# Rope tables of a hybrid transformer layer: their last operations on a scratch unit taken in the ninth pair

## The chip, the cores and the metric

One core of a Trainium2 chip. The metric is device time in microseconds of one execution of the whole layer. Its engines run queues of their own: TensorE (PE, with PEld for its weight loads), VectorE (DVE), ScalarE (ACT), GpSimd (POOL) and SyncE (SP, which issues the loads).

## The reference

One layer on x (1 x 512 tokens x 1024, float32): a half-weighted SwiGLU feed-forward block (width 2816), a mixing stage with two groups of heads, a second half-weighted SwiGLU block, a final RMSNorm. Cut to what matters:

```python
x = x + FFN_RES * swiglu(rms_norm(x, ffn1_norm[l]), ffn1_w_gate[l], ffn1_w_up[l], ffn1_w_down[l])
u = rms_norm(x, mix_norm[l]) @ w_in[l]
c_q, c_kv, k_rope, mq, mk, mv = jnp.split(u, cuts, axis=-1)
a_out = mla_attention(c_q, c_kv, k_rope, positions, ...)      # 8 heads, rotary part of 32
b_out = moba_attention(mq..., mk..., mv..., positions)        # 8 heads, ALiBi
x = x + jnp.concatenate([a_out, b_out], axis=-1) @ w_out[l]
x = x + FFN_RES * swiglu(rms_norm(x, ffn2_norm[l]), ...)
return rms_norm(x, final_norm)

def apply_rope(x, pos):
    inv = jnp.power(ROPE_BASE, -jnp.arange(half) * 2.0 / r)
    ang = pos[:, :, None, None] * inv
    cos, sin = jnp.cos(ang), jnp.sin(ang)
    ...
```

The rope tables are the cosines and sines of position times frequency, for 512 positions and 16 frequencies: 128 partitions of 4 x 16 values. Positions are an input, so the tables are computed on the chip: the angle is reduced to the range from -pi to pi in several pieces, clipped to ±3.1415925, and the sine taken of it (for the sine) and of pi/2 - |angle| (for the cosine).

## The kernel before

Every float32 matrix product is done as three products of a high and a low half: ACT copies a weight chunk of 128 x 1024 into the high half (line 251, in `split`), DVE or POOL subtracts to get the low half (line 252), and PE multiplies (`mm3`, or line 485 in `product`). SP loads the chunks from HBM (line 236).

The up and gate matrices of a feed-forward block are done in `gate_up`: a first piece in `fm_half`, and then ten pairs, each of seven `product`s of 24 matmuls (a scheme with seven products of blocks instead of eight). Before a product, `pump` writes down the splits of the chunks of up to four products ahead; between products `pair` evacuates the banks on ACT (line 495) and DVE (lines 511 to 527), with a Silu on ACT (lines 514, 525). The sums of weight blocks that the scheme wants are DVE's (lines 292 to 300).

Scratch comes from `scr`, nine units of 128 x 512 in one tile. `ualloc` takes the unit at the head of the free list, `ufreeit` puts one back at its tail. Unit 8 is set aside for `blk`, the block of rope tables. Each pair takes three units, called u1, u5 and u2 (with their contents s1, s5 and s2), and gives all three back.

Work that no product needs at once is given as a generator in `aside`; every `product` ends with `tick(2)`, which runs two of its steps. `gate_up` of the first block puts `rope_tables` there when the fourth pair begins (j == 3); ahead of its last part it steps idly until `state["late"]`, which is set from the ninth pair on (j >= 8). It holds one unit for all its 64-column pieces (a, t2, t1, n, p, q, z, y). Nearly all of it is on POOL: the angles (line 794), the reduction in pieces (lines 832 to 849 with the helper lines 787, 788), the clip (line 852). The last part is |a| on DVE (line 857), pi/2 - |a| on POOL (line 859), three Sines on ACT (lines 862, 864, 866), a negation and a memset on POOL (lines 868, 870). The tables are first read in the mix stage, in `c_evac` and `rope_transpose`.

The program so written is not the order of the queues: a planner, when the program is built, orders each engine's instructions by its own estimate of when each can start, keeps what depends on data and on buffers, gives earlier lines of the program precedence, and puts semaphores between engines. On the chip each engine runs its queue in that order.

Of the kernel before, what the change touches and what calls it, by code (L numbers as in the profile page):

```python
# [14 lines left out]
AF = mybir.ActivationFunctionType  # L15
OP = mybir.AluOpType
# [24 lines left out]
def _cut(v):  # L41
    b = np.array([v], np.float32).view(np.uint32) & 0xfffff000
    return float(b.view(np.float32)[0])
# [9 lines left out]
def layer_kernel(ctx, tc, xt, xtok, pos_row, pos_tok, gains, fin, consts, w, wc, out):  # L53
    nc = tc.nc
    V, A, G, T = nc.vector, nc.scalar, nc.gpsimd, nc.tensor
# [90 lines left out]
    def ualloc():  # L146
        u = ufree.popleft()
        return u, scr[:, u * 512:(u + 1) * 512]

    def ufreeit(u):  # L150
        ufree.append(u)
# [627 lines left out]
    blk = scr[:, (NU - 1) * 512:].rearrange("p (t c) -> p t c", t=4)  # L779

    def rope_tables():
        u, sc = ualloc()
        tl = [sc[:, i * 64:i * 64 + 64] for i in range(8)]
        a, t2, t1, n, p, q, z, y = tl

        def STT(o, a_, c, b_, op0, op1):
            G.tensor_scalar(y, a_, c, 1.0, op0=op0, op1=OP.mult)
            G.tensor_tensor(o, y, b_, op=op1)

        pf = sm[:, 68:72]  # L790
        V.tensor_copy(pf, pi)
        yield 1
        v3 = a.rearrange("p (t f) -> p t f", t=4)
        G.tensor_tensor(v3, pf[:, :, None].to_broadcast([128, 4, 16]),
                        cst[:, None, CINV - C0:CINV - C0 + 16].to_broadcast([128, 4, 16]), op=OP.mult)
        yield 1

        def reduce(x):
            G.tensor_scalar(n, x, 1.0 / _P, MAGIC, op0=OP.mult, op1=OP.add)
            yield 1  # L800
            G.tensor_scalar(n, n, -MAGIC, 1.0, op0=OP.add, op1=OP.mult)
            yield 1
            for c in (PI_A, PI_B, PI_C):
                STT(x, n, -c, x, op0=OP.mult, op1=OP.add)
                yield 1

        def fold(t, x, step):

            d = math.fmod(step, _P)
            d = d - _P if d > math.pi else d  # L810
            da = _cut(d)
            db = _cut(d - da)
            dc = d - da - db
            G.tensor_scalar(n, t, da / step / _P, MAGIC, op0=OP.mult, op1=OP.add)
            yield 1
            G.tensor_scalar(n, n, -MAGIC, 1.0, op0=OP.add, op1=OP.mult)
            yield 1
            G.tensor_scalar(x, t, da / step, 1.0, op0=OP.mult, op1=OP.mult)
            yield 1
            STT(x, n, -PI_A, x, op0=OP.mult, op1=OP.add)  # L820
            yield 1
            STT(x, t, db / step, x, op0=OP.mult, op1=OP.add)
            yield 1
            STT(x, n, -PI_B, x, op0=OP.mult, op1=OP.add)
            yield 1
            STT(x, t, dc / step, x, op0=OP.mult, op1=OP.add)
            yield 1
            STT(x, n, -PI_C, x, op0=OP.mult, op1=OP.add)
            yield 1

        m2, m1 = MAGIC * 2.0 ** 21, MAGIC * 2.0 ** 12
        G.tensor_scalar(t2, a, m2, 1.0, op0=OP.add, op1=OP.mult)
        yield 1
        G.tensor_scalar(t2, t2, -m2, 1.0, op0=OP.add, op1=OP.mult)
        yield 1
        G.tensor_tensor(a, a, t2, op=OP.subtract)
        yield 1
        G.tensor_scalar(t1, a, m1, 1.0, op0=OP.add, op1=OP.mult)
        yield 1
        G.tensor_scalar(t1, t1, -m1, 1.0, op0=OP.add, op1=OP.mult)  # L840
        yield 1
        G.tensor_tensor(a, a, t1, op=OP.subtract)
        yield 1
        yield from reduce(a)
        yield from fold(t1, p, 2.0 ** 12)
        yield from fold(t2, q, 2.0 ** 21)
        G.tensor_tensor(p, p, q, op=OP.add)
        yield 1
        G.tensor_tensor(a, a, p, op=OP.add)
        yield 1  # L850
        yield from reduce(a)
        G.tensor_scalar(a, a, 3.1415925, -3.1415925, op0=OP.min, op1=OP.max)
        yield 1

        while not state["late"]:
            yield 1
        V.scalar_tensor_tensor(z, a, -1.0, a, op0=OP.mult, op1=OP.max)
        yield 1
        G.tensor_scalar(z, z, -1.0, math.pi / 2, op0=OP.mult, op1=OP.add)
        yield 1  # L860
        z3 = z.rearrange("p (t f) -> p t f", t=4)
        A.activation(blk[:, :, 64:80], z3, AF.Sin)
        yield 1
        A.activation(blk[:, :, 80:96], z3, AF.Sin)
        yield 1
        A.activation(blk[:, :, 112:128], v3, AF.Sin)
        yield 1
        G.tensor_scalar(blk[:, :, 96:112], blk[:, :, 112:128], -1.0, 1.0, op0=OP.mult, op1=OP.mult)
        yield 1
        G.memset(blk[:, :, 0:64], 1.0)  # L870
        yield 1
        ufreeit(u)
# [8 lines left out]
    def dist_tables():  # L881
# [30 lines left out]
        for i in range(4):  # L912
# [10 lines left out]
            yield 1  # L923

    gate_up(c_f1, c_s1, start_mid0, start_mid1, rope_tables)
    down(c_d1, 8)
    close_part()
# [495 lines left out]
    for t in range(4):  # L1423
        u, xg = ualloc()
        v = v0[:, t:t + 1]
        for n, (a, b) in enumerate(parts[t]):
            for c in last:
# [3 lines left out]
                                   op0=OP.mult, op1=OP.add)  # L1431
# [8 lines left out]
        w1, w2, y, z = tv[:, t:t + 1], tv[:, 4 + t:5 + t], rstd[:, t:t + 1], tt[:, t:t + 1]  # L1440
# [103 lines left out]
```

## Time and profile before

| | |
|---|---|
| median of three runs | 953.11 us (951.67 to 954.19) |
| profiled execution, its own time | 952.19 us |
| span of that execution | 950.4 us |
| mean granted TensorE clock | 0.989 |
| PE busy, share of the span | 920.2 us, 97% |
| DVE busy | 748.6 us, 79% |
| ACT busy | 517.4 us, 54% |
| POOL busy | 116.7 us, 12% |

The span runs from the first to the last instruction; the execution's own time has 1.8 us more around it. Busy times are sums over the whole span; the span is cut into 40 slices of 23.8 us in the page's second part, where a digit is the busy share of a slice in tenths. A wait is named as "engine, line waiting <- engine, line that released it".

### The profile page before, as it was taken

The page shows a single profiled execution, that of the slowest core. Times are in us where ns is not written, and L with a number is a line of the kernel's source. Part 1 is how long each engine was busy: PE and PEld are TensorE (multiplying, and loading weights), DVE is VectorE, ACT ScalarE, POOL GpSimd, SP SyncE. Part 2 cuts the span into 40 slices and gives each one's busy share as a digit, 9 for nine tenths or more (in the row PEclk, how much of TensorE's full clock was granted, in tenths as well). Part 3 has the DMA queues.
Part 4 walks back from the last instruction along what each step waited for, and adds up shares of the span by engine and source line. Part 5 has one row for each costly group of instructions (what it writes and reads, how often), then busy time and mean ns, then how long its engine had stood idle before and what let it go on. Part 6 is the DMA issues. An engine that isn't in the chain of part 4 may idle for free.

```text
span 950.4 us, 15102 instructions
## 1 busy us (share of the span) xinstructions
PE 920.2 (97%) x5901; PEld 838.1 (88%) x5901; DVE 748.6 (79%) x1090; ACT 517.4 (54%) x832; POOL 116.7 (12%) x173
## 2 busy tenths in 40 slices
PE   8993999999999999999999999999999999999997
PEld 6993999999988888998787888899999999988886
DVE  6984989879988956445688887689798879988845
ACT  7643544545636525455787865655455544735524
POOL 2053000000000000011756730000000000000001
PEclk9997999999999999999999999999999999999999
DMA  9420433224603424132434362123233323610302
GB/s 329 174 89 24 133 112 112 90 91 152 220 5 100 118 89 138 62 126 72 152 121 152 125 195 98 45 69 109 90 93 127 114 89 112 221 67 26 109 0 89
DMA packets 38088, 105.41 MB, mean 111 GB/s; under 512 B 4480, under 2 KB 11264, under 8 KB 38016
## 3 DMA queue, kind: packets, MB, share of 16 engines
q1 hardware_dynamic: 37008, 102.61, 33.2%
q10 hardware_dynamic: 1008, 1.84, 0.5%
q8 instruction: 46, 0.75, 0.3%
q14 instruction: 26, 0.21, 0.1%
HBM read 90.40 MB, written 2.10 MB: 97 GB/s over the span
## 4 chain that ended last, share of the span: by engine, by line
PE 46%; ACT 2%; DVE 1%; POOL 1%; DMA 1%; issue 0%; ACTq 0%; SPq 0%; DVEq 0%; POOLq 0%
PE bank L485 21%; PE bank L326 7%; PE bank L328 7%; PE bank L327 7%; PE bank L1190 2%; PE bank L1172 1%; POOL scr L1143 1%; ACT scr L1135 1%; DMA ext<-scr 0%; PE bank L402 0%; ACT ar L251 0%; DMA ar<-scr 0%; DVE ext L1176 0%; ACT ar L1175 0%; POOL ext L1259 0%
## 5 line engine op out<-in xcount | busy, mean ns | idle before, releaser
L485 PE MATMUL bank<-ar 128*128 128x256 f32 x3360 | 406.6, 284 | 16.6 <-DVE scr L516 16.0
L485 PEld LDWEIGHTS bank<-ar 128*128 128x128 f32 x3360 | 405.2, 193 | 17.7 <-DVE scr L516 16.4
L251 ACT ACTIVATE ar<-raw 128x1024 fp32r<-128x1024 f32 (+3 forms) x182 | 177.0, 982 | 155.3 <-issue 45.5
L326 PE MATMUL bank<-ar 128*128 128x512 f32 (+4 forms) x664 | 255.3, 385 | 2.6 <-ACT ar L251 2.2
L328 PE MATMUL bank<-ar 128*128 128x512 f32 (+4 forms) x664 | 253.7, 382 | 0.0
L327 PE MATMUL bank<-ar 128*128 128x512 f32 (+4 forms) x664 | 253.6, 382 | 0.0
L252 DVE TENSOR_TENSOR ar<-raw,ar 128x1024 fp32r<-128x1024 f32 (+2 forms) x164 | 192.0, 1181 | 53.9 <-ACT ar L251 35.8
L326 PEld LDWEIGHTS bank<-ar 128*128 128x128 f32 x664 | 124.8, 188 | 25.9 <-ACT ar L251 2.6
L328 PEld LDWEIGHTS bank<-ar 128*128 128x128 f32 x664 | 125.1, 188 | 23.3
L327 PEld LDWEIGHTS bank<-ar 128*128 128x128 f32 x664 | 125.2, 188 | 22.4 <-DVE ar L390 0.2
L251 ACT ACTIVATE ar<-sq 128x1024 fp32r<-128x1024 f32 x62 | 65.6, 1058 | 77.4 <-DVE sq L295 27.1
L252 DVE TENSOR_TENSOR ar<-sq,ar 128x1024 fp32r<-128x1024 f32 x62 | 75.6, 1220 | 26.8 <-ACT ar L251 26.8
L1409 POOL TENSOR_TENSOR x<-x,tabs 128x512 f32<-128x512 f32 x4 | 5.2, 1288 | 353.6 <-ACT scr L354 353.6
L1143 POOL TENSOR_SCALAR scr<-scr,sm 128x128 f32<-128x128 f32 (+1 forms) x64 | 41.1, 662 | 41.4 <-DVE sm L1140 40.5
L617 DVE SCALAR_TENSOR_TENSOR x<-bank,sm,x 128x512 f32<-128x512 f32 x37 | 27.0, 747 | 23.8 <-PE bank L328 23.8
L1135 ACT ACTIVATE scr<-scr,sm 128x256 f32<-128x256 f32 (+1 forms) x64 | 35.3, 553 | 16.9 <-DVE sm L1127 16.8
L495 ACT ACTIVATE scr<-bank 128x512 f32<-128x512 f32 x60 | 34.9, 581 | 6.7 <-PE bank L485 6.7
L354 ACT ACTIVATE scr<-x 128x512 f32<-128x512 f32 x28 | 17.5, 631 | 29.2 <-DVE x L617 27.0
L948 POOL MEMSET ext<- 64x512 f32 x6 | 3.3, 547 | 215.0 <-DVE ar L252 214.5
L575 ACT ACTIVATE ar<-h 128x512 fp32r<-128x512 f32 x28 | 17.3, 630 | 17.1 <-PE bank L327 8.8
L252 POOL TENSOR_TENSOR ar<-raw,ar 128x512 fp32r<-128x512 f32 x18 | 24.1, 1351 | 9.2 <-ACT ar L251 8.3
L295 DVE TENSOR_TENSOR sq<-sq,raw 128x1024 f32<-128x1024 f32 x20 | 24.5, 1223 | 0.5
(239 smaller groups left out, 926.8 us busy)
## 6 DMA issues: line engine op xcount, KB each, us to landing
raw<-in_w_dram SPq DMA_DIRECT2D x144, 512.0 KB, 3.5
h<-in_w_dram SPq DMA_DIRECT2D x8, 512.0 KB, 3.5
ext<-scr SPq DMA_DIRECT2D x13, 256.0 KB, 2.4
raw<-in_wc_dram SPq DMA_DIRECT2D x8, 336.0 KB, 3.3
ext<-scr SPq DMA_DIRECT2D x13, 192.0 KB, 2.3
x<-in_xtok_dram SPq DMA_DIRECT2D x4, 512.0 KB, 8.2
ext<-scr SPq DMA_DIRECT2D x16, 128.0 KB, 2.1
xs<-in_xt_dram SPq DMA_DIRECT2D x5, 256.0 KB, 5.0
```

The lines of the kernel that those rows point to most:

```text
L251: A.activation(sl(h)[:, a:b], src[:, a:b], AF.Copy)
L252: (e or V).tensor_tensor(sl(l)[:, a:b], src[:, a:b], slf(h)[:, a:b], op=OP.subtract)
L295: V.tensor_tensor(sq, sq, r(q11), op=OP.subtract)
L326: T.matmul(ps, lhsT=ah, rhs=bh, start=start, stop=False, **kw)
L327: T.matmul(ps, lhsT=ah, rhs=bl, start=False, stop=False, **kw)
L328: T.matmul(ps, lhsT=al, rhs=bh, start=False, stop=stop, **kw)
L485: T.matmul(o, lhsT=a_[:, ws], rhs=b_[:, xs_], start=first and e == 0 and k == 0 and n == 0, stop=k == 3 and n == 2, skip_group_check=True)
L495: A.activation(t, banks[b], AF.Copy)
L617: V.scalar_tensor_tensor(xs, banks[b], r, xs, op0=OP.mult, op1=OP.add)
L1135: A.activation(p, p, AF.Exp, scale=-1.0, bias=mn[z][:, i:i + 1], accum_out=rs[z][:, i:i + 1])
L1143: G.tensor_scalar(p, p, ri[z][:, i:i + 1], 1.0, op0=OP.mult, op1=OP.mult)
L1190: T.matmul(banks[b][:, 128 * j:512], lhsT=vw, rhs=pr[:, o:o + n], start=(j == 0 and e == 0), stop=(j == 3 and e == 1))
```

## The change

The name z for the seventh piece of the old unit goes. The clip, which wrote a in place and stood ahead of the loop that waits for the ninth pair, moves behind that loop, and writes to a piece e of a unit that is taken there (u2 in the generator, not the u2 of a pair). |e| and pi/2 - |e| are made in a second piece of that unit, and the second of the two operations goes from POOL to DVE. The third Sine reads e instead of a. The new unit is given back behind the third Sine, the old one at the end as before.

```diff
-        a, t2, t1, n, p, q, z, y = tl
+        a, t2, t1, n, p, q, _, y = tl
...
         yield from reduce(a)
-        G.tensor_scalar(a, a, 3.1415925, -3.1415925, op0=OP.min, op1=OP.max)
-        yield 1
 
         while not state["late"]:
             yield 1
-        V.scalar_tensor_tensor(z, a, -1.0, a, op0=OP.mult, op1=OP.max)
-        yield 1
-        G.tensor_scalar(z, z, -1.0, math.pi / 2, op0=OP.mult, op1=OP.add)
-        yield 1
-        z3 = z.rearrange("p (t f) -> p t f", t=4)
+        u2, sc = ualloc()
+        e, z = sc[:, 0:64], sc[:, 64:128]
+        e3, z3 = (x.rearrange("p (t f) -> p t f", t=4) for x in (e, z))
+        G.tensor_scalar(e, a, 3.1415925, -3.1415925, op0=OP.min, op1=OP.max)
+        yield 1
+        V.scalar_tensor_tensor(z, e, -1.0, e, op0=OP.mult, op1=OP.max)
+        yield 1
+        V.tensor_scalar(z, z, -1.0, math.pi / 2, op0=OP.mult, op1=OP.add)
+        yield 1
         A.activation(blk[:, :, 64:80], z3, AF.Sin)
         yield 1
         A.activation(blk[:, :, 80:96], z3, AF.Sin)
         yield 1
-        A.activation(blk[:, :, 112:128], v3, AF.Sin)
-        yield 1
+        A.activation(blk[:, :, 112:128], e3, AF.Sin)
+        yield 1
+        ufreeit(u2)
         G.tensor_scalar(blk[:, :, 96:112], blk[:, :, 112:128], -1.0, 1.0, op0=OP.mult, op1=OP.mult)
```

## The prediction

> **What bounds the kernel now.** The page first: its head, busy times and slices.
>
> ```profile
> span 950.4 us, 15102 instructions
> ...
> PE 920.2 (97%) x5901; PEld 838.1 (88%) x5901; DVE 748.6 (79%) x1090; ACT 517.4 (54%) x832; POOL 116.7 (12%) x173
> ...
> PE   8993999999999999999999999999999999999997
> ...
> PEclk9997999999999999999999999999999999999999
> ```
>
> TensorE is busy for 97% of the span, so time can come only from the 30 us in which it is not. One slice stands out, the fourth (71 to 95 us): PE busy 3 tenths, granted clock 7 tenths. The waits of PE say how much of the 30 us is one wait, the first row here:
>
> ```profile
> PE bank L485 <- DVE scr L516: 16.0, 2, 15.1
> PE bank L326 <- ACT ar L251: 2.2, 1, 2.2
> ```
>
> Half of PE's idle time is a single wait of 15.1 us in the first feed-forward block. The timeline of all engines there tells its cause; the number in brackets is the idle time ahead of a row and what ended it:
>
> ```profile
> 54.79 0.68 DVE L517 TENSOR_TENSOR h<-scr 128x512 f32<-128x512 f32 x1
> ...
> 55.56 1.20 POOL L794 TENSOR_TENSOR scr<-sm,cst 128x64 f32<-128x64 f32 x1 [41.69 <-DVE h L517]
> ...
> 61.95 1.40 POOL L842 TENSOR_TENSOR scr<-scr 128x64 f32<-128x64 f32 x1
> ...
> 62.26 0.60 ACT L495 ACTIVATE scr<-bank 128x512 f32<-128x512 f32 x1 [0.70 <-PE bank L485]
> ...
> 67.90 1.34 DVE L297 TENSOR_TENSOR raw<-raw,raw 128x1024 f32<-128x1024 f32 x1
> 68.25 1.10 POOL L787 TENSOR_SCALAR scr<-scr 128x64 f32<-128x64 f32 x1
> 69.43 0.32 POOL L788 TENSOR_TENSOR scr<-scr 128x64 f32<-128x64 f32 x1
> ...
> 82.71 0.24 POOL L852 TENSOR_SCALAR scr<-scr 128x64 f32<-128x64 f32 x1
> 82.98 0.26 ACT L866 ACTIVATE scr<-scr 128x64 f32<-128x64 f32 x1 [20.13 <-POOL scr L852]
> 83.15 1.04 ACT L251 ACTIVATE ar<-sq 128x1024 fp32r<-128x1024 f32 x1
> ...
> 84.22 1.23 DVE L252 TENSOR_TENSOR ar<-sq,ar 128x1024 fp32r<-128x1024 f32 x1 [14.97 <-ACT ar L251]
> ...
> 85.36 0.69 DVE L516 TENSOR_TENSOR scr<-bank,scr 128x512 f32<-128x512 f32 x1
> ...
> 86.10 26.13 PE L485 MATMUL bank<-ar 128*128 128x256 f32 x204 [15.12 <-DVE scr L516]
> ...
> 99.60 0.22 DVE L857 SCALAR_TENSOR_TENSOR scr<-scr 128x64 f32<-128x64 f32 x1
> ...
> 99.91 1.15 POOL L859 TENSOR_SCALAR scr<-scr 128x64 f32<-128x64 f32 x1 [16.34 <-DVE scr L857]
> 101.09 0.26 ACT L862 ACTIVATE scr<-scr 128x64 f32<-128x64 f32 x1 [1.31 <-POOL scr L859]
> ```
>
> Three things are to be read here. First, the engines' queues are not in program order: the rope generator starts in the fourth pair of the code and its Sin L866 is written in the ninth, yet POOL starts the tables at 55.56, as soon as DVE L517 of the first pair has let go of the scratch unit, and ACT holds L866 already in the second pair. The planner pulls an operation forward as far as its data and its buffer allow. Second, each queue runs in its order: ACT has nothing to show from 62.86 (62.26 + 0.60) to 82.98, because L866 stands at its head and waits for the clip L852 at the end of POOL's chain. Third, the chain of the stall: clip, Sin, ACT's weight copy L251, DVE's subtraction L252, DVE's bank evacuation L516, and the seventh product of the second pair, which adds to that bank. DVE idles 14.97 us and PE 15.12 us, for one operation of 0.26 us that nobody needs before the mix stage.
>
> **The change, part by part.** *The clip and the third Sin.* Before, the clip wrote its own unit, so only the POOL chain held it. Now it writes a unit taken when the ninth pair's first product has been written down. Followed through the code, the free list (nine units, one set aside for the table block, one held by the rope scratch, three taken and given back by each pair) then has at its head number 7, last used as s1 of the sixth pair, whose last reader is L527 of that pair. L527 writes to the h tiles in the first six pairs only, so the last of these is the one:
>
> ```profile
> L527 DVE TENSOR_TENSOR h<-bank,scr x6: 677/686/692, 61.4 to 173.5; 128x512 f32<-128x512 f32 x6
> ```
>
> As L794 waited for L517, the clip must now wait for this L527, at 173.5 in the old time, some 158 in the new. No Sin can be pulled ahead of the clip, since all three read what it writes. The stall at 71 us therefore loses its cause.
>
> *What of the 15.12 us comes back.* What is late next is DVE itself, which was busy up to 69.24 (67.90 + 1.34). Without the Sin, L251's input from DVE is there and L252 follows at 69.24 where it stood at 84.22: everything behind it moves by 14.97 us or so, L516 ends at 71.1 and PE, done at 70.98 (86.10 - 15.12), waits 0.14 us instead. Gain: 14.98 us.
>
> *The clock after the gap.* The windows (length, then busy time of PE, PEld, DVE, ACT, POOL, then granted clock, DMA share, GB/s):
>
> ```profile
> 55.00:71.00 16.00, 15.98 (x134) 15.77 (x132) 14.24 (x15) 5.51 (x7) 14.01 (x19) 1.00 0.40 132
> 71.00:86.00 15.00, 0.00 (x0) 0.00 (x0) 1.78 (x3) 2.67 (x4) 9.42 (x35) 0.65 0.00 1
> 86.00:90.00 4.00, 3.90 (x21) 3.90 (x22) 4.00 (x6) 1.06 (x1) 0.00 (x0) 0.59 0.36 113
> 90.00:94.00 4.00, 4.00 (x36) 4.00 (x35) 3.17 (x5) 3.10 (x5) 0.00 (x0) 1.00 0.06 23
> ...
> 152.00:252.00 100.00, 100.00 (x834) 99.96 (x833) 89.59 (x101) 55.36 (x71) 0.00 (x0) 1.00 0.43 137
> ...
> 86.10:251.62 165.52, 165.52 (x1367) 165.52 (x1368) 147.97 (x163) 88.42 (x110) 1.15 (x1) 0.99 0.39 124
> ```
>
> and, from the chain that ended last, the second block, which runs the same ten pairs with no rope tables beside them:
>
> ```profile
> 638.25 192.95 PE bank L485 x1608
> ```
>
> The clock falls to 0.59 and is back at 1.00 from 90 us on. The second block needs 192.95/1608 = 0.1200 us a matmul; the 1368 after the gap (1680 in ten pairs of seven products of 24, less the thirteen products up to the gap) should take 164.16 us and took 165.52. So 1.36 us more go with the gap. TensorE: Matmul & The Clock Gate (Part 1: The HAM clock gate) of the Trainium skill says that an idle window of about 3.4 us drops the clock to half, and about as long a busy one restores it; an estimate by that figure is half of 3.4, 1.7 us, which would put the result 0.34 us lower. The second block's row also shows no stall in the same code with nothing of the tables in the queues.
>
> *POOL's chain beside a busy DVE.* From 69.24 to 84.22 DVE stood idle, and POOL's operations took 0.24 to 0.32 us; beside DVE they had taken up to 1.40 (L842). After the change DVE does not stop. Of the chain, 14 operations lay before 69.35 (to the end of L787 at 68.25) and 37 before the clip come after: 5 up to 71 us (19 - 14), and 32 of the second window's 35, less one on the border, L868 and the clip. At the early pace, (69.35 - 55.56)/14 = 0.985 us, they end at 106 us; at 1.40 us each plus 0.1 between them, at 125. Both are well ahead of 158. What they cost DVE, by its groups in 55 to 69 us (with POOL) and in 102 to 250 us (without):
>
> ```profile
> L252 DVE TENSOR_TENSOR ar<-raw,ar 128x1024 fp32r<-128x1024 f32 x4 | 5.0, 1286 | 0.0
> L297 DVE TENSOR_TENSOR raw<-raw,raw 128x1024 f32<-128x1024 f32 x2 | 2.6, 1280 | 0.0
> ...
> L252 DVE TENSOR_TENSOR ar<-raw,ar 128x1024 fp32r<-128x1024 f32 x32 | 38.8, 1220 | 4.3 <-ACT ar L251 4.3
> ...
> L297 DVE TENSOR_TENSOR raw<-raw,raw 128x1024 f32<-128x1024 f32 x6 | 7.3, 1221 | 0.1
> ```
>
> 4 x 0.066 + 2 x 0.059 = 0.38 us for 14 POOL operations, 0.027 each: 1.0 us for 37. From above, L297 at 67.90 took 1.34, 0.12 longer: 4.4 us for 37. DVE idles 10.4 us of 100 with the pairs at full speed (152 to 252), 3.8 us in the chain's 36, so PE loses between 0 and 0.6 us. I take 0.4, nearer the upper end because DVE enters this stretch with no lead (busy without a break up to 69.24).
>
> *The last operations at their new place.* The clip moves behind L527; SP's queue is not passed, no DMA moves. POOL has nothing else in its queue till the mix stage. ACT's Sins may wait for the clip, or for DVE's second step, as L862 did at 101.09: 1.31 us, PE at work throughout. Behind a waiting Sin are ACT's copies, then DVE's subtractions, then products several steps on. Bounds 0 and 1.31 us; I take 0, because that row cost PE nothing. The z step goes from POOL (1.15) to DVE, where its neighbour L857 took 0.22: it fits in DVE's 10.4 us. The three Sins, the memset and the negation stay as many.
>
> *The free list.* One more unit is out for part of a pair that needs three of seven. The order differs through the down projection and is the same four units (7, 6, 8, 5) where attention starts. Cost 0.
>
> Sum on the profiled execution: 952.19 - 14.98 - 1.36 + 0.4 = 936.25 us. The median shown, 953.11, is 0.92 above that execution; so 937.2 us.
>
> **The rivals.** *VectorE becomes the bound while the chain runs.* For it, PE's other wait on L516, at the end of the first pair, where DVE had no slack either:
>
> ```profile
> 53.80 17.18 PE L485 MATMUL bank<-ar 128*128 128x256 f32 x141 [0.85 <-DVE scr L516]
> ```
>
> Against: 0.027 us an operation. If DVE stood still for every POOL operation at its undisturbed 0.32 us, 37 cost 11.8, less 3.8 of slack: 8.0 us instead of 0.4, 944.8. It decides from 0.1 us an operation up. SBUF — State Buffer (SBUF: two separate sides) of the Trainium skill speaks for this: the port pair of the two engines is locked for a whole instruction and the loser blocks fully. By that the trace agrees for POOL (0.24 against 1.40) and shows little of it for DVE.
>
> *The wait moves instead of going.* ACT's order is fixed by a planner that thought the chain finished soon after 62.86 and was 20 us off. If a Sin stands in the sixth or seventh pair ahead of what releases it, ACT stops again; with one operation left on POOL, not 52, the error is 1.15 us and a hand-over, 1.31 us as at L862, on ACT and once more for DVE's steps: 2.6 us, 939.8; a gap over that would need an order that I cannot see, up to 950.
>
> *The change does not do it:* if the unit were free at 82 us already, clip and Sin would stay put: 953.1. It would take a unit last used in the second pair; the list gives the sixth.
>
> *Slower.* If POOL's chain still ran when L527 of the sixth pair is through, Sin L866's successor would hold ACT as before, and longer: to lose 3 us against now, the stall must pass 18 us, the chain end after 175 us, and its 37 operations take (175 - 69.4)/37 = 2.9 us each, twice the longest row. Time then 956 or more.
>
> **How the numbers follow.** Forecast 0.74 (934 to 939.5). VectorE bound 0.09 (939.5 to 945). The wait moved 0.09 (939.5 to 950). No effect 0.04. Slower 0.04. A run of this kernel is told from no change beyond about 0.3%, 2.9 us: faster 0.91, same 0.05, slower 0.04. Range 934 to 943: it leaves out the upper parts of the two partial rivals and the last two cases, some 0.17.
>
> **What would show it.** PE's waits should have no entry above 2.5 us; the fourth slice should read 9 for PE and clock; L252 should run at about 69 us without idle time before it; POOL's chain should last till 95 to 125 us with operations of about 1 us; POOL's clip should be released by DVE L527 near 158 us, the Sins after it. The prediction is wrong if a Sin holds ACT for over 3 us anywhere, if the new PE idle time in the second to fourth pair passes 2 us, or if stages behind the first block, which I take as unmoved, change their length.

## The result, and the profile after

The changed kernel takes 936.03 us (median of four runs, 934.88 to 936.12) against 952.75 of the kernel before (four runs, one more than in the table ahead): a ratio of 0.9822, 95% interval 0.981 to 0.9833. The forecast was 937.2. The profiled execution took 936.12 us, 16.07 less than the one before it; the sum made for that execution was 936.25.

The page of the changed kernel, the lines that answer to those shown of before:

```profile
span 934.3 us, 15098 instructions
...
PE 918.2 (98%) x5901; PEld 835.8 (89%) x5901; DVE 751.7 (80%) x1091; ACT 518.0 (55%) x832; POOL 138.7 (15%) x172
...
PE   8999999999999999999999999999999999999997
...
PEclk9999999999999999999999999999999999999999
```

The hole in the fourth slice is gone from PE's row and from the clock's. POOL is 22 us busier with one instruction less: its operations are the same but for the one that went to DVE, and now they run beside a DVE at work. PE's longest waits in the whole span are these:

```profile
PE bank L326 <- DVE ar L1261: 1.4, 2, 1.0
PE bank L326 <- ACT ar L251: 1.3, 1, 1.3
...
PE bank L485 <- DVE scr L516: 0.8, 1, 0.8
```

The wait of 15.1 us for L516 has left the list; what remains under that name is the first pair's 0.8. The timeline of the changed kernel, from its views by engine, shows the new order (lines behind 852 have moved: the clip is L858, |e| L860, pi/2 - |e| L862, the third Sine L868):

```profile
67.23 1.06 ACT L251 ACTIVATE ar<-sq 128x1024 fp32r<-128x1024 f32 x1 [4.57 <-DVE sq L292]
...
67.70 1.34 DVE L297 TENSOR_TENSOR raw<-raw,raw 128x1024 f32<-128x1024 f32 x1
68.96 1.25 DVE L252 TENSOR_TENSOR ar<-sq,ar 128x1024 fp32r<-128x1024 f32 x1
70.14 0.68 DVE L516 TENSOR_TENSOR scr<-bank,scr 128x512 f32<-128x512 f32 x1
...
53.60 181.58 PE L485 MATMUL bank<-ar 128*128 128x256 f32 x1508 [0.83 <-DVE scr L516]
...
102.70 1.17 POOL L788 TENSOR_TENSOR scr<-scr 128x64 f32<-128x64 f32 x1
157.71 2.21 POOL L858 TENSOR_SCALAR scr<-scr 128x64 f32<-128x64 f32 x1 [53.84 <-DVE h L527]
159.95 0.26 ACT L868 ACTIVATE scr<-scr 128x64 f32<-128x64 f32 x1 [1.03 <-POOL scr L858]
159.95 0.23 DVE L860 SCALAR_TENSOR_TENSOR scr<-scr 128x64 f32<-128x64 f32 x1
160.21 0.20 DVE L862 TENSOR_SCALAR scr<-scr 128x64 f32<-128x64 f32 x1
```

DVE goes from L297 to L252 without a pause where it stood for 14.97 us. PE runs from 53.60 to the end of the block, 1508 matmuls, with no entry in its waits. POOL's chain ends at 103.87. The clip waits 53.84 us on an engine that has nothing else to do, and is let go by DVE L527 of the sixth pair at 157.7. ACT waits 1.03 us for it, and nothing follows from that.

Where the time came from: in the first block from PE's restart in the first pair to the end of the tenth, 181.41 us (53.60 to 235.01) against 197.82 (53.80 to 251.62), 16.41 less. That is the wait of 15.12 and 1.29 more. Ahead of it 0.20 us were gained; the first block's down projection and the mix stage gave 0.51 us back (378.08 us from 235.01 to 613.09, against 377.57); and the second block's pairs and the tail did not change: 321.21 us in both.

### The profile page after: what moved, and what is told of

It reads as the page before. It is cut to its first block, busy times and chain, and to the rows that moved or that the text cites. A ratio compares the mean times of both kernels' runs of the same rounds, so it can differ in the third digit from the quotient of the medians.

```text
span 934.3 us, 15098 instructions
## 1 busy us (share of the span) xinstructions
PE 918.2 (98%) x5901; PEld 835.8 (89%) x5901; DVE 751.7 (80%) x1091; ACT 518.0 (55%) x832; POOL 138.7 (15%) x172
## 4 chain that ended last, share of the span: by engine, by line
PE 44%; ACT 3%; DVE 2%; issue 2%; POOL 2%; DMA 0%; ACTq 0%; DVEq 0%; POOLq 0%
PE bank L485 22%; PE bank L326 7%; PE bank L327 7%; PE bank L328 7%; PE bank L1193 1%; ACT scr L1138 1%; POOL scr L1146 1%; PE bank L1175 1%; POOL ar L252 0%; ACT ar L251 0%; DVE ext L1179 0%; PE bank L402 0%; DMA ar<-scr 0%; ACT scr L1202 0%; DMA ext<-scr 0%
## 5 line engine op out<-in xcount | busy, mean ns | idle before, releaser
L252 DVE TENSOR_TENSOR ar<-raw,ar 128x1024 fp32r<-128x1024 f32 (+2 forms) x164 | 192.3, 1182 | 54.3 <-ACT ar L251 35.5
L252 DVE TENSOR_TENSOR ar<-sq,ar 128x1024 fp32r<-128x1024 f32 x62 | 75.8, 1223 | 10.2 <-ACT ar L251 10.1
L495 ACT ACTIVATE scr<-bank 128x512 f32<-128x512 f32 x60 | 34.9, 581 | 6.3 <-PE bank L485 6.3
L252 POOL TENSOR_TENSOR ar<-raw,ar 128x512 fp32r<-128x512 f32 x18 | 23.5, 1320 | 9.2 <-ACT ar L251 8.3
L297 DVE TENSOR_TENSOR raw<-raw,raw 128x1024 f32<-128x1024 f32 x20 | 24.5, 1225 | 0.2
```

The source lines that it names most:

```text
L252: (e or V).tensor_tensor(sl(l)[:, a:b], src[:, a:b], slf(h)[:, a:b], op=OP.subtract)
L297: V.tensor_tensor(r(q21), r(q11), r(q21), op=OP.subtract)
L495: A.activation(t, banks[b], AF.Copy)
```

## Experiments

Two accounts stood against each other. The theory: the late release of the new unit holds back the clip and, through the data, the Sines; nothing else of the change matters. Its rivals: the operations' new place in the program, the second buffer as such, or the step that went from POOL to DVE. The ratios are to the kernel before on the same chip, where its median was 952.49 to 953.01 us. The changed kernel itself was not run again there; its 936.03 stands beside, good to the half microsecond by which those medians differ.

**Program place alone** (no new unit):

```diff
-        u2, sc = ualloc()
-        e, z = sc[:, 0:64], sc[:, 64:128]
+        e, z = a, tl[6]
...
-        ufreeit(u2)
```

> The changed kernel, but the clip stays in place in the old unit and |e| and pi/2 - |e| in the old unit's seventh piece: the operations are written down in the ninth pair, the second step is on DVE, no new unit is taken. Theory (the late release of the new unit pins the clip and with it the Sines): nothing pins them now, ACT takes the third Sine in the second pair again, PE waits about 15 us for L516, 952 to 954 us. Rival (the place in the program, behind the loop for the ninth pair, is what moves them): as the changed kernel, about 936 us, no wait of PE over 2 us in the first block.

Measured: 952.96 us, ratio 0.9996 (0.9984 to 1.0007). The clip and the Sine are written down in the ninth pair and run in the second all the same. From its POOL, ACT and PE timelines:

```profile
83.01 0.24 POOL L857 TENSOR_SCALAR scr<-scr 128x64 f32<-128x64 f32 x1
83.28 0.26 ACT L867 ACTIVATE scr<-scr 128x64 f32<-128x64 f32 x1 [20.10 <-POOL scr L857]
86.40 165.65 PE L485 MATMUL bank<-ar 128*128 128x256 f32 x1367 [15.10 <-DVE scr L516]
```

The place in the program is worth nothing.

**The unit taken at the generator's start:**

```diff
         u, sc = ualloc()
+        u2, s2_ = ualloc()
...
-        u2, sc = ualloc()
-        e, z = sc[:, 0:64], sc[:, 64:128]
+        e, z = s2_[:, 0:64], s2_[:, 64:128]
```

> The changed kernel, but its new unit is taken where the generator starts, in the fourth pair, where the list gives a unit last used in the first pair. Theory: the unit is free before POOL's chain ends, so it pins nothing: stall of about 15 us as before, 952 to 954 us. Rival (a second unit as such, or the separate buffer that does away with working in place, is enough): about 936 us.

Measured: 952.88 us, ratio 0.9998 (0.9986 to 1.0009), PE's wait for L516 15.15 us. A second buffer that is free early pins nothing.

**The step on DVE alone**, in the kernel before:

```diff
-        G.tensor_scalar(z, z, -1.0, math.pi / 2, op0=OP.mult, op1=OP.add)
+        V.tensor_scalar(z, z, -1.0, math.pi / 2, op0=OP.mult, op1=OP.add)
```

> The kernel before with one part of the change alone: pi/2 - |a| on DVE instead of POOL. Theory: the third Sine still stands at ACT's head in the second pair: 951 to 954 us, PE wait of 15 us for L516; ACT's wait of 1.31 us for POOL at 101 us becomes a shorter one for DVE and costs nothing either way. Rival (the step on POOL is what the Sines wait for): several us faster.

Measured: 953.0 us, ratio 0.9999 (0.9988 to 1.0009). ACT's wait at 101.78 is 1.31 us for DVE instead of 1.31 for POOL. Here the expected shorter wait did not come.

**All but that step**, in the changed kernel:

```diff
-        V.tensor_scalar(z, z, -1.0, math.pi / 2, op0=OP.mult, op1=OP.add)
+        G.tensor_scalar(z, z, -1.0, math.pi / 2, op0=OP.mult, op1=OP.add)
```

> The changed kernel, with pi/2 - |e| back on POOL. Theory: the move to DVE is worth nothing: 936 us, within 1 us of the changed kernel; ACT waits up to 1.3 us more for POOL at about 160 us, PE does not. Rival (the hand-over DVE, POOL, ACT at the new place costs what it takes): 1.0 to 2.6 us more, 937 to 939 us.

Measured: 935.4 us (935.1 to 935.82), ratio 0.9816 (0.98 to 0.9832). ACT waits 0.56 us for POOL where it waited 0.23 for DVE; PE sees neither. With the run before, the step is out of the account. Its runs lie within the changed kernel's own 934.88 to 936.12, so it is no faster either.

**A unit released at another time.** Without the loop that waits for the ninth pair, the unit is taken in the sixth:

```diff
-        while not state["late"]:
-            yield 1
```

> The changed kernel without the loop that waits for the ninth pair: the unit is taken in the sixth pair, as soon as the chain is written down; the list then gives a unit last read by L527 of the fourth pair, about 115 us in the changed kernel's time, after the chain's end at 104 us. Theory: no stall, clip released by DVE L527 near 115 us, 935 to 938 us. Rival (the lateness of the ninth pair is what counts): a stall of some size comes back, 940 us or more.

Measured: 935.77 us (two runs), ratio 0.9812 (0.9784 to 0.9841). The clip is at the place that the list gives:

```profile
115.84 1.08 POOL L856 TENSOR_SCALAR scr<-scr 128x64 f32<-128x64 f32 x1 [11.82 <-DVE h L527]
```

So the ninth pair has no merit of its own; any release behind the chain's end does. And a release ahead of it, with the unit taken at the end of the fourth pair:

```diff
         yield from reduce(a)
+        u2, s2_ = ualloc()
         yield from fold(t1, p, 2.0 ** 12)
...
-        u2, sc = ualloc()
-        e, z = sc[:, 0:64], sc[:, 64:128]
+        e, z = s2_[:, 0:64], s2_[:, 64:128]
```

> The changed kernel, but the new unit is taken at the end of the fourth pair, behind the first reduction: the list gives a unit last read by L527 of the second pair, about 77 us in the changed kernel's time, 27 us before the chain's end. Theory: the Sine is held back to about 79 us only, ACT waits there for the rest of the chain, DVE runs dry some 5 us later and POOL then goes at its undisturbed pace to about 92 us: a stall of PE of 5 to 10 us and a cold clock behind it, 941 to 950 us. Rival (it is all or nothing: pinned or not): 936 or 953 us.

Measured: 947.92 us, ratio 0.9945 (0.9922 to 0.9969). The Sine waits at another place and for less long, as its ACT and PE timelines show:

```profile
91.02 0.26 ACT L868 ACTIVATE scr<-scr 128x64 f32<-128x64 f32 x1 [12.05 <-POOL scr L858]
92.76 154.69 PE L485 MATMUL bank<-ar 128*128 128x256 f32 x1272 [10.11 <-ACT scr L495]
```

It is not all or nothing: the stall is the time by which POOL's chain is late for the Sine's place in ACT's queue, less what PE still has in hand (2 to 5 us in these kernels). PE's 10.11 us are just above the 5 to 10 expected. Behind the Sine stood a bank evacuation on ACT itself (L495), one hand-over nearer to PE than the weight copy of the kernel before, and PE's gap was 1.94 us shorter than ACT's wait (12.05) in place of 5.01 (20.13 against 15.12).

**The same from the chain's side.** The kernel before with a shorter chain (the folds of the angle's high parts left out):

```diff
-        yield from fold(t1, p, 2.0 ** 12)
-        yield from fold(t2, q, 2.0 ** 21)
-        G.tensor_tensor(p, p, q, op=OP.add)
-        yield 1
-        G.tensor_tensor(a, a, p, op=OP.add)
-        yield 1
```

> The kernel before, without the two folds and their sums (the same 28 operations left out). Theory (the stall's length is the lag of POOL's chain behind the place where the planner put the Sine): the chain ends at about 70 us instead of 82.7, PE stands for 5 to 7 us instead of 15.1, 940 to 946 us. Rival (the stall is a matter of the queue's order alone, whatever POOL does): 952 us.

Measured: 943.88 us (two runs), ratio 0.991 (0.9892 to 0.9928).

```profile
70.90 0.26 ACT L860 ACTIVATE scr<-scr 128x64 f32<-128x64 f32 x1 [9.14 <-POOL scr L846]
71.70 171.71 PE L485 MATMUL bank<-ar 128*128 128x256 f32 x1416 [6.40 <-ACT scr L495]
```

And the changed kernel with a longer one, first by 48 operations and then by 112:

```diff
+        for _ in range(6):     # 14 in the second kernel
+            for _ in reduce(a):
+                pass
         while not state["late"]:
```

> The changed kernel with the last reduction done six times more (48 more operations on POOL, which change nothing in the angles). Theory: POOL's chain lasts till about 149 us at 0.93 us an operation, ahead of the unit's release at 158 us, so ACT is not held; DVE's operations get longer beside POOL for 45 us more, at 0.03 to 0.06 us for each of POOL's, 1.4 to 2.9 us, inside the 4 to 5 us that DVE idles there: 936 to 937 us. Rival (VectorE is the bound while the chain runs): at 0.32 us an operation 10 us more, 941 to 946 us.

> The changed kernel with the last reduction done fourteen times more (112 more operations on POOL). Theory: the chain is still running when L527 of the sixth pair lets go of the unit, so the Sine holds ACT from about 158 us as it did at 63: DVE runs dry some 6 us later with about 47 operations left, which then take 0.36 us each, to 181 us; PE stands for 15 to 20 us and goes on cold: 950 to 960 us. Rival (in the ninth pair's place a waiting Sine is harmless): 936 to 938 us.

Measured: 935.96 us (0.9819, 0.9804 to 0.9834) with 48 more, 952.51 us (0.9994, 0.9984 to 1.0005) with 112 more. The first kernel's clip still waits for DVE, the second's Sine for POOL:

```profile
142.14 1.17 POOL L788 TENSOR_TENSOR scr<-scr 128x64 f32<-128x64 f32 x1
157.85 2.21 POOL L861 TENSOR_SCALAR scr<-scr 128x64 f32<-128x64 f32 x1 [14.54 <-DVE h L527]
```

```profile
175.85 0.26 ACT L871 ACTIVATE scr<-scr 128x64 f32<-128x64 f32 x1 [17.37 <-POOL scr L861]
177.13 73.57 PE L485 MATMUL bank<-ar 128*128 128x256 f32 x600 [14.41 <-ACT scr L495]
```

With the release fixed at 157.8, a chain that ends at 143 costs nothing and one that ends at 175 brings the whole stall back, in the sixth and seventh pairs. That is the mechanism of the rival "slower", made by hand: its place was right. In the kernel as changed the chain would have to end 54 us later before it delays the clip at all. The chain's pace was overestimated: 48 operations took 39.4 us (103.9 to 143.3), 0.82 each and not 0.93.

**What the chain costs beside a busy DVE.** The changed kernel without the same folds:

> The changed kernel without the two folds of the angle's high parts and the two sums behind them (28 of POOL's 52 operations left out; for positions under 4096 those parts are zero). It measures what POOL's chain beside a busy DVE still costs. Theory: nothing that PE sees, 935.5 to 936.5 us, within 0.5 us of the changed kernel. Rival (VectorE bound while the chain runs): 1 to 4 us faster.

Measured: 935.67 us, ratio 0.983 (0.9817 to 0.9844). The median is 0.36 under the changed kernel's, the ratio a little above its 0.9822: no difference. Windows of DVE with POOL at work (48 operations more) and without, from 104 to 143 us of the two kernels:

```profile
104.00:143.00 39.00, 39.00 (x328) 39.00 (x327) 35.55 (x36) 18.74 (x23) 34.93 (x49) 1.00 0.36 116
```

```profile
104.00:143.00 39.00, 39.00 (x328) 39.00 (x327) 34.89 (x37) 18.64 (x24) 0.00 (x0) 1.00 0.40 122
```

The busy time of DVE is 0.66 us longer, but for one operation less (36 against 37). Put side by side, the same 36 operations took 37.69 us with POOL at work and 36.49 without (sums of their durations, which overlap a little): 1.20 us for 48 operations, 0.025 each. DVE still idles 3.4 us. Where the chain itself runs in the changed kernel, 69 to 105 us, DVE's group of weight subtractions reads:

```profile
L252 DVE TENSOR_TENSOR ar<-raw,ar 128x1024 fp32r<-128x1024 f32 x8 | 10.0, 1284 | 0.0
```

That is 64 ns over the 1220 of an undisturbed one; with the other groups' excess DVE loses 1.5 us there to 37 operations, 0.04 each. There DVE is idle for only 0.5 of the 36 us, but PE has no wait: VectorE does not become the bound.

**The clock term.** Twice PE was given work in the gap of the kernel before, ahead of the last product of the second pair:

```diff
+        if late_fill and j == 2:           # first block only; 110, then 127 matmuls
+            d = balloc()
+            h, l = tq["t4"]
+            for k in range(late_fill):
+                T.matmul(banks[d][:, 0:256], lhsT=sl(h)[:, 0:128], rhs=sl(h)[:, 256:512], start=True, stop=True)
+            bfree.append(d)
         product(cs[6], b, "t4", False)
```

> The kernel before, with 110 matmuls of 256 columns into a spare bank ahead of the second pair's last product: PE has 13.2 us of work (110 x 0.120) in the 15.1 us in which it stood, and nothing else is moved. Theory (about 1.4 us of the gain is the clock, which drops to 0.59 after the gap): granted clock 1.00 throughout, the matmuls behind the gap at 0.120 instead of 0.121 us, 951.4 us, 1.0 to 1.6 us under the kernel before. Rival (the slow matmuls after the gap wait for DVE and not for the clock): no gain, 952.5 to 953 us.

Measured with 110: 952.52 us, ratio 0.9997 (0.9989 to 1.0006): no gain. PE stood for 2.15 us behind the added work, and the clock fell just as after 15 us:

```profile
71.00:86.00 15.00, 13.27 (x111) 13.07 (x109) 1.46 (x2) 2.67 (x4) 9.74 (x35) 1.00 0.01 2
86.00:90.00 4.00, 3.58 (x17) 3.58 (x18) 4.00 (x6) 1.06 (x1) 0.00 (x0) 0.58 0.28 86
```

> As with 110 matmuls, but 127 of them (127 x 0.1215 = 15.4 us), so that PE has work from its last product up to the moment at which L516 lets it go on: there PE was left idle for 2.15 us behind its 13.36 us of work, and the clock fell to 0.58 behind that gap all the same, so the term was not taken out. Theory (1.4 us of the gain is the clock): with a gap under 0.5 us the clock stays at 1.00 from 86 to 90 us, the matmuls behind run at 0.120 us, 951.0 to 951.6 us, if PE does not wait for DVE instead. Rival (the first matmuls behind the gap are held by DVE's results, and the clock's fall costs nothing by itself): new waits of PE for DVE or ACT of 1 to 2 us between 86 and 100 us, and 952 to 953 us.

Measured with 127: 953.06 us, ratio 1.0006 (0.9997 to 1.0015): no gain either.

```profile
86.00:90.00 4.00, 4.00 (x34) 4.00 (x35) 4.00 (x6) 1.09 (x2) 0.00 (x0) 1.00 0.32 128
90.00:94.00 4.00, 4.00 (x36) 4.00 (x35) 3.96 (x5) 2.04 (x5) 1.16 (x1) 1.00 0.11 23
94.00:98.00 4.00, 2.28 (x19) 2.08 (x18) 3.97 (x5) 3.83 (x6) 0.00 (x0) 0.97 0.30 116
98.00:102.00 4.00, 4.00 (x23) 4.00 (x23) 2.01 (x2) 0.60 (x1) 0.00 (x0) 0.60 0.71 236
```

```profile
PE bank L485 <- ACT scr L495: 1.7, 1, 1.7
```

With the gap filled, 34 matmuls ran from 86 to 90 us instead of 21 and the clock was 1.00. But PE then met a wait of 1.7 us for ACT at 95 us, behind which the clock fell to 0.60. The added matmuls had also changed DVE's and ACT's order there, so the two can't be set against each other cleanly. The outcome is the one that the rival foretold, a new wait of 1 to 2 us and 952 to 953 us; but with the order changed the test is inconclusive on whether the kernel before would have been 1.4 us faster with a full clock behind its gap. What the other kernels show is that each gap costs more than its length. The first 4 us behind the gap, of the short chain, the unit of the fourth pair, the long chain, the kernel before and the unit taken early:

```profile
71.70:75.70 4.00, 4.00 (x20) 4.00 (x21) 4.00 (x5) 1.58 (x2) 0.00 (x0) 0.56 0.00 0
```

```profile
92.76:96.76 4.00, 4.00 (x18) 4.00 (x19) 3.23 (x5) 0.83 (x3) 0.00 (x0) 0.50 0.00 0
```

```profile
177.13:181.13 4.00, 4.00 (x22) 4.00 (x23) 3.04 (x4) 2.46 (x4) 0.00 (x0) 0.62 0.00 0
```

```profile
86.10:90.10 4.00, 4.00 (x21) 4.00 (x22) 4.00 (x5) 1.06 (x1) 0.00 (x0) 0.61 0.38 118
```

```profile
86.06:90.06 4.00, 4.00 (x18) 4.00 (x19) 4.00 (x6) 1.06 (x1) 0.00 (x0) 0.50 0.35 121
```

| profiled execution | PE's gap, us | from its end to the end of the ten pairs, us | matmuls there x 0.1200 us | difference, us |
|---|---|---|---|---|
| before, short chain | 6.40 | 171.55 | 169.92 | 1.63 |
| unit of the fourth pair | 10.11 | 154.52 | 152.64 | 1.88 |
| changed, chain longer by 112 | 14.41 | 73.40 | 72.00 | 1.40 |
| before | 15.12 | 165.52 | 164.16 | 1.36 |
| program place alone | 15.10 | 165.48 | 164.16 | 1.32 |
| unit taken early | 15.15 | 166.84 | 164.16 | 2.68 |
| before, step on DVE | 15.09 | 166.84 | 164.16 | 2.68 |

The fourth column takes the second block's 0.1200 us a matmul, as the prediction does. PE is busy in the whole of each of these stretches, and away from the gap the granted clock is 1.00; so the difference is what the slow clock takes: 1.3 to 2.7 us, whether the gap is 6 or 15 us long. It isn't the same in every execution: of the last four rows, with one and the same stall, two had a clock of 0.61 in the first 4 us and lost 1.3 to 1.4 us, two had 0.50 and lost 2.7.

## Why the prediction was right

*The cause of the stall and its removal:* right, and shown by taking the pin away (952.96), putting it early (952.88), moving it (935.77, 947.92) and outrunning it (952.51). The unit that the list was said to give, released by L527 of the sixth pair near 158 us, is the one in the trace, at 157.7.

*14.98 us from the wait:* L252 follows L297 at 68.96 and L516 ends at 70.82. The 0.14 us of wait kept in the sum do not appear in PE's waits.

*1.36 us from the clock:* the block gained 1.29 us beyond the wait, and the granted clock is 1.00 from 71 to 112 us. The size holds for this execution; other executions of the same stall lost 2.68, so another profile would have put another number into the sum. That the clock alone makes the difference is supported by the table and not isolated.

*0.4 us for POOL beside DVE:* POOL's chain ended at 103.9 where 106 was forecast, with operations of up to 1.40 us. DVE lost 0.025 to 0.04 us an operation, at the lower of the bounds (0.027 and 0.12), and PE lost nothing: the block's 1512 matmuls at 0.1200 us are 181.44 us, and it took 181.41. Taking 28 operations out changed nothing either. This was the term with the most doubt, and its 0.4 did not appear. The page SBUF — State Buffer (SBUF: two separate sides) of the Trainium skill, by whose lock the loser blocks fully for a whole operation, is met by the trace on POOL's side only (up to 1.40 us beside a busy DVE); DVE's 0.025 to 0.04 us are far from a whole POOL operation of 0.24 us and more.

*The last operations at 0:* ACT waited 1.03 us for the clip and 0.23 for DVE, both inside 1.31, and PE waited for neither.

*Stages behind the block unmoved:* wrong. The down projection and the mix stage got 0.51 us longer, nearly all of it PE idle time in small pieces (3.94 us against 3.44). A changed length there was one of the prediction's own signs of being wrong, and the prediction had put it at nothing. The same stretch took between 376.86 and 378.86 us in the other kernels' profiles; the engines' orders in it may have changed with the free list, but the cause is not shown.

*The sum, and from the execution to the median:* the sum for the execution was 0.13 us off, and that is luck in part. In the block the terms make 15.94 us (14.98 + 1.36 - 0.4), 0.47 less than the 16.41 measured; the 0.20 us gained ahead of it stood in no term, and the 0.51 lost behind it made up for most of both. The median was 1.2 us off. The 0.92 us by which the first median lay above its profiled execution was carried over, and did not recur: the changed kernel's profiled execution lies 0.09 above its median.

## What to carry to other kernels

Where a planner orders the queues, as here, the place of a line in the program need not keep a side task away from the main work; in these runs only data and buffers did. An operation that waits on a slow engine should be tied to a buffer that comes free after the slow chain's end, and the margin read from the trace (54 us here), because a longer chain brings the stall back. Look for the engine whose head of queue waits on an idle-looking side chain: 0.26 us of work held three engines for 15 to 20.

## What the runs showed of the hardware

The clock fell after gaps shorter than expected: to 0.58 behind one of 2.15 us and to 0.60 behind one of 1.72 us. In the profiles of all fourteen kernels it fell behind each wait of PE of 1.72 us or more, and behind none of up to 1.69 us: the short chain's wait of 1.69 us at 6.95 was followed by a clock of 1.00, and the wait of 1.82 us at the same place in the kernel with the program place alone by one of 0.62 over the next 4 us. TensorE: Matmul & The Clock Gate (Part 1: The HAM clock gate) of the Trainium skill gives an idle window of about 3.4 us; these runs show falls with half of that idle. Whether a fixed limit lies between 1.69 and 1.72 us, or these few waits only happen to divide there, they don't settle.

And POOL's clip took 2.21 us for 128 x 64 values beside a DVE at work in the changed kernel, 1.08 in the one without the loop, against 0.24 beside an idle DVE.
